# Merge gates through DRAM and a new order of the mixers in a hybrid decoder trunk

## The chip, the cores and the metric

The kernel runs on one core of a Trainium2 chip. The metric is the device time of one execution in microseconds; several runs are taken and the median is compared.

## The reference

Two layers (DEPTH = 2) work on 256 prompt positions and 8 sample sequences of 8 positions, 320 columns in all, of width 1024. Each layer is:

```python
x = x + 0.5 * swiglu_ffn(rmsnorm(x), ...)            # 1024 -> 2 x 2816 -> 1024
h = rmsnorm(x)
q, k, v, g_ret, u, z, xbc, dt, gate_logits = split(h @ w_in)
y_ret = (silu(g_ret) * norm(retention(rotary(q), rotary(k), v, state))) @ ret_w_o   # 4 heads
y_s5  = glu(gelu(grouped complex scan of u) @ s5_w_glu)                              # 64 groups
y_ssd = norm(silu(z) * (ssd(silu(conv(xbc)), softplus(dt), state) + d * xs)) @ ssd_w_o   # 4 groups of 8 heads
gates = sigmoid(gate_logits)                          # 3 x 1024 channels
x = x + (gates[0] * y_ret + gates[1] * y_s5 + gates[2] * y_ssd) @ w_out
x = x + 0.5 * swiglu_ffn(rmsnorm(x), ...)
```

All is float32. The outputs are the activations and the new states of the retention, S5, SSD and convolution branches.

## The kernel before

Activations lie transposed: a tile `t` is 128 channels by 320 positions (53 such buffers). Every large product is made exact enough by splitting both operands into a high and a low part: `stream` (L265) loads weights in pieces of 128x1024 (512 KB) on SP's queue, ScalarE rounds them (`whi`, L278) and VectorE takes the rest (`wlo`, L279), and `proj` (L285) issues three matmuls for each of eight blocks (L292 to L294), so a projection unit is 24 matmuls of 128x320 into one of four PSUM buffers `pp`. The smaller matmuls of the branches go to four PSUM buffers `pb`.

A scheduler sorts the instructions of each engine: it takes the order in which the program emits them as precedence, and issues what is ready by its cost model. `high_priority` moves an instruction forward by a number of places (AHEAD for weight loads and splits, SOON for PSUM evictions). The program emits the mixer with `weave` (L379): a list of main units (projections), and after each unit a share of the steps of the side generators (the branches).

The stages of a mixer, in `layer` (L1278): the opening (time steps `ssd_dt`, S5 inputs `u`, the convolution inputs x of SSD group 0); then, for g = 0 to 3, the SSD group g (`ssd_group`, L588) beside the x of the next group, the z gates (`ssd_gate`, L748) of the group before and that group's part of the SSD output projection (`ssd_part`, L552); retention's q, k and v units stand with the last groups. Then the four retention heads (`ret_head`, L836) run two at a time beside the third merge gate (`g2`), the retention gates (`ret_gate`, L920) and the first merge gates; the S5 blocks (`s5_block`, L1172) run beside all of these from group 2 on. Last come the retention output projection, the second merge gates with `s5_post`, the S5 output projection with its merge, and `w_out`.

A merge gate (`gate`, L1270) is one projection unit and a Tanh; its tile stays in SBUF until the merge. POOL's queue issues, in its order, all loads and stores but the weights': states (L601, L842), row sums that are broadcast (L596), S5 tables (L1183 to L1189), results (L703, L909, L1241, L1256).

Of the kernel before, what the change touches and what calls it, by code (L numbers as in the profile page):

```python
# [40 lines left out]
SOON = 60  # L41
# [3 lines left out]
DTL = 3  # L45
URAW = 6
NPRI = 200
AHEAD = 120
# [105 lines left out]
class Trunk:  # L154
# [270 lines left out]
    DT_STEPS = 5  # L425

    def ssd_dt(self, l, h, r):
        nc, C = self.nc, self.C
        resets = self.tab(7)
        p = self.proj(self.stream("w_dt", l), h)  # L430
# [7 lines left out]
        nc.vector.tensor_scalar(y, y, 0.0, None, op0=ALU.max)  # L438
        z = self.t()
# [9 lines left out]
        dt = self.t()  # L449
        nc.vector.scalar_tensor_tensor(dt, q, 2.0, y, op0=ALU.mult, op1=ALU.add)  # L450
        ea = self.s("ea", [128, 1])
        nc.scalar.activation(ea, self.col(l, "a_log", 0), AF.Exp)
        dta = self.t()
        nc.vector.tensor_scalar(dta, dt, ea, -1.0, op0=ALU.mult, op1=ALU.mult)
        cum = self.t()
        nc.vector.tensor_tensor_scan(cum, resets, dta, initial=0.0, op0=ALU.mult, op1=ALU.add)
        cd = self.dr.tile([128, T], F32, name=self.nm("cd"))
# [6 lines left out]
        nrev = self.t()  # L464
# [6 lines left out]
        w = self.t()  # L471
        nc.scalar.activation(w[:, :128], nrev[:, :128], AF.Exp, scale=-1.0, bias=cum[:, LP - 1:LP])
        nc.scalar.activation(w[:, 128:], nrev[:, 128:], AF.Exp, scale=-1.0)
        nc.vector.tensor_tensor(w, w, dt, op=ALU.mult)
# [10 lines left out]
        yield  # L485
# [4 lines left out]
        yield  # L490
# [95 lines left out]
    SSD_STEPS = 18  # L586

    def ssd_group(self, l, g, xin):  # L588
# [3 lines left out]
        bcs = []  # L592
# [6 lines left out]
        h0 = [self.A(2, 512) for _ in range(4)]  # L599
        for i in range(4):  # L600
            nc.gpsimd.dma_start(out=h0[i], in_=ap["ssm_in"][l][:, g, 2 * i:2 * i + 2])  # L601
# [194 lines left out]
    def ret_v(self, l, h, v, vs):  # L796
# [4 lines left out]
        def unit(nh):  # L801
# [20 lines left out]
            for b in range(2):  # L822
                nc.scalar.activation(vt[:, b], pv[b], AF.Copy)

            nc.scalar.activation(vt[:NS, 2], pv[2][:NS], AF.Copy)
            nc.vector.tensor_tensor(vt[NS:, 2], pv[2][NS:], vt[:NS, 2], op=ALU.add)
            v.append(vt)
            VS = self.A(2, 512, dt=F32R)
            self.spread(self.stack(vt[NS:, 2], "vh"), 0, VS)
            vs.append(VS)  # L830

        return [lambda nh=nh: unit(nh) for nh in range(2)]

    RET_STEPS = 8

    def ret_head(self, l, hd, rot, v, vs, out):  # L836
# [6 lines left out]
        mk, qd = self.tab(2 + hd), self.tab(6)  # L843
        q, k = rot["q", hd], rot["k", hd]
# [66 lines left out]

        pm = self.ps()
# [4 lines left out]
        out[hd] = os, self.rstd(os, 256)  # L917
        yield

    def ret_gate(self, l, h, hd, st, heads):  # L920

        nc = self.nc

        def unit(e):
            pg = self.proj(st, h())
            sg = self.t()
            nc.scalar.activation(sg, pg[:, :T], AF.Silu)
            os, r = heads[hd]
            nc.vector.scalar_tensor_tensor(os[e], sg, self.col(l, "ret_ln_g", 2 * hd + e), os[e], op0=ALU.mult, op1=ALU.mult)
            nc.vector.tensor_tensor(os[e], os[e], r, op=ALU.mult)  # L930

        return [lambda e=e: unit(e) for e in range(2)]
# [237 lines left out]
    S5_STEPS = 8  # L1170

    def s5_block(self, l, Q, ud, yd, blk):  # L1172
# [20 lines left out]
        cs, sn = (rt[:, 512 * i:512 * i + 512].rearrange("p (g k) -> p g k", g=NG) for i in range(2))  # L1193
        yield
# [82 lines left out]

    def layer(self, l):  # L1278
# [28 lines left out]
        rest = xi[NRAW:]
        for m in range(len(ui)):
            rest.insert(2 * m + 1, ui[m])
        self.weave(rest, (dt, self.DT_STEPS - 1 - DTL))  # L1310
# [10 lines left out]
        gu = [[lambda i=i: gs[i].append(self.gate(S[f"t{i}"], h())) for m in range(KD)] for i in range(2)]
        GD = (0, 0, 0, 0, 0, 2, 4, 2)
        GO = [sum(GD[:i]) for i in range(9)]
        G = lambda i: gu[0][GO[i]:GO[i + 1]]
        PL = ((), (), (0,), (1, 2), (3, 4), (5, 6), (7,))
        P = lambda i: [s5(*PL[i])] if PL[i] else []
        self.weave(uu + xu(1) + G(0), [(dt, DTL), ssd(0)], *P(0))
        XK = 2
        mix = lambda a, b: a[:XK] + b + a[XK:]
        self.weave(mix(xu(2), zu(0)) + G(1) + ou(0), ssd(1), *P(1))  # L1330
        self.weave(mix(xu(3), zu(1)) + G(2) + ou(1)[:4] + [self.ret_tabs] + ou(1)[4:], ssd(2), *P(2))
        self.weave(mix(qk, zu(2)) + G(3) + ou(2), ssd(3), *P(3))
        self.weave(vu[:1] + zu(3) + vu[1:] + G(4) + ou(3), *P(4))
        ret = [(self.ret_head(l, hd, rot, v, vs, heads), self.RET_STEPS) for hd in range(RH)]

# [5 lines left out]
        rg = lambda hd: self.ret_gate(l, h, hd, S["g"], heads)  # L1341
        self.weave(g2 + G(5), ret[:2], *P(5))
        self.weave(rg(0) + rg(1) + G(6), ret[2:], *P(6))
        for u in rg(2) + rg(3):
            u()
        yret = [self.split(o) for hd in range(RH) for o in heads[hd][0]]
        for u in G(7):
            u()
# [181 lines left out]
```

## Time and profile before

| | |
|---|---|
| median of 3 runs | 2414.15 us (2404.64 to 2421.31) |
| profiled execution | 2408.9 us |
| its span | 2407.1 us |
| TensorE busy | 2302.3 us (96%) in 15798 matmuls |
| VectorE busy | 1752.1 us (73%) |
| ScalarE busy | 1256.8 us (52%) |
| POOL busy | 392.3 us (16%) |
| mean granted TensorE clock | 0.982 |
| moved by DMA | 439.88 MB, 183 GB/s |

The times of the busy rows are unions: matmuls overlap, so the sum of their single durations (about 0.31 us each) is more than the busy time. A granted clock of 1.00 is 2.4 GHz and 0.50 is 1.2 GHz; means between them are mixtures of the two. Layer 0's mixer lies from 253 to 962 us and layer 1's from 1443 to 2170 us; the rest are the feed-forward parts.

### The profile page before, as it was taken

To read this page: it belongs to the slowest core of one execution; us is meant where nothing else is said; L and a number is where in the kernel's file an instruction comes from. 1 tells how busy PE (TensorE), PEld (TensorE's weight loads), DVE (VectorE), ACT (ScalarE), POOL (GpSimd) and SP (SyncE) were. 2 spreads that over 40 slices of the span, in tenths; PEclk is the share of its full clock that TensorE was granted. 3 is DMA by queue.
4 is the path that set the end of the run, shared out by engine and by line. 5 is a ranking of instruction groups with operands and counts; after the bars stand their busy time and mean duration, and the time that the engine had idled before them with its cause. 6 is when DMAs were issued, how large, how long until landed. Compare 5 with 4: busy or idle time off the path is not lost.

```text
span 2407.1 us, 41311 instructions
## 1 busy us (share of the span) xinstructions
PE 2302.3 (96%) x15798; PEld 2182.7 (91%) x15798; DVE 1752.1 (73%) x3366; ACT 1256.8 (52%) x2281; POOL 392.3 (16%) x762
## 2 busy tenths in 40 slices
PE   7999999989999999999999999899899999999998
PEld 7999887868788999999999999788788889999998
DVE  7989789888765656776877677988786666566564
ACT  4444478767444454444443445788565444544342
POOL 0111233221122100000100113432111321000000
PEclk9999999999999999999999999999999999999999
DMA  5767656664566555555556566665655755555553
GB/s 170 233 211 226 213 173 219 193 226 132 177 221 213 151 161 177 146 165 177 176 177 191 180 210 191 204 208 163 203 160 178 255 191 154 174 151 149 149 149 110
DMA packets 126247, 439.88 MB, mean 183 GB/s; under 512 B 18208, under 2 KB 22016, under 8 KB 126048
## 3 DMA queue, kind: packets, MB, share of 16 engines
q1 hardware_dynamic: 82080, 293.11, 40.4%
q0 software_dynamic: 43968, 144.12, 17.9%
q8 instruction: 124, 2.03, 0.4%
q14 instruction: 75, 0.61, 0.1%
HBM read 373.45 MB, written 65.03 MB: 182 GB/s over the span
## 4 chain that ended last, share of the span: by engine, by line
PE 80%; ACT 6%; DVE 6%; DMA 4%; issue 3%; POOL 1%; SPq 0%; DVEq 0%; ACTq 0%; POOLq 0%
PE pp L292 23%; PE pp L293 23%; PE pp L294 22%; ACT whi L278 2%; DVE wlo L279 1%; DMA t<-in_tabs 1%; ACT B L661 1%; PE pb L1199 1%; PE pb L689 1%; PE pb L348 1%; PE pb L333 1%; PE pb L1247 1%; DMA A<-toep 1%; PE pp L818 1%; PE pb L708 1%
## 5 line engine op out<-in xcount | busy, mean ns | idle before, releaser
L292 PE MATMUL pp<-t,whi 128*128 128x320 f32 x4304 | 1347.5, 314 | 34.0 <-ACT t L363 12.7
L294 PE MATMUL pp<-t,wlo 128*128 128x320 f32 x4304 | 1339.2, 312 | 7.9 <-DVE wlo L279 7.9
L293 PE MATMUL pp<-t,whi 128*128 128x320 f32 x4304 | 1340.6, 312 | 1.1 <-DVE t L303 0.7
L278 ACT ACTIVATE whi<-wraw 128x1024 fp32r<-128x1024 f32 x554 | 585.9, 1058 | 760.5 <-PE pp L293 374.5
L279 DVE TENSOR_TENSOR wlo<-wraw,whi 128x1024 fp32r<-128x1024 f32 x554 | 676.7, 1222 | 260.1 <-ACT whi L278 258.1
L292 PEld LDWEIGHTS pp<-t,whi 128*128 128x128 f32 x4304 | 813.4, 189 | 50.2 <-ACT whi L278 16.2
L294 PEld LDWEIGHTS pp<-t,wlo 128*128 128x128 f32 x4304 | 813.0, 189 | 16.1 <-DVE wlo L279 11.4
L293 PEld LDWEIGHTS pp<-t,whi 128*128 128x128 f32 x4304 | 814.3, 189 | 6.4 <-DVE t L303 1.6
L302 ACT ACTIVATE t<-t 128x320 fp32r<-128x320 f32 x184 | 83.7, 461 | 57.0 <-DVE t L1367 28.9
L303 DVE TENSOR_TENSOR t<-t,t 128x320 fp32r<-128x320 f32 x184 | 88.7, 486 | 22.5 <-ACT t L302 21.7
L526 DVE SCALAR_TENSOR_TENSOR acc<-xpad,cols,acc 128x344 f32<-128x344 f32 x144 | 81.0, 571 | 5.8 <-ACT acc L523 4.5
L403 DVE TENSOR_TENSOR t<-pp,t 128x320 f32<-128x320 f32 x88 | 42.6, 485 | 44.8 <-PE pp L294 39.0
L409 DVE TENSOR_TENSOR t<-t,pp 128x320 f32<-128x320 f32 x88 | 42.6, 484 | 38.6 <-PE pp L294 37.7
L323 ACT ACTIVATE t<-t 128x320 f32<-128x320 f32 x104 | 47.6, 462 | 32.4 <-DVE t L916 16.0
L661 ACT ACTIVATE B<-C,tk 128x128 f32<-128x128 f32 x192 | 63.2, 392 | 0.1
L414 DVE SCALAR_TENSOR_TENSOR t<-pp,t 128x320 f32<-128x320 f32 x64 | 31.2, 488 | 35.2 <-PE pp L294 35.0
L404 ACT ACTIVATE t<-t 128x320 f32<-128x320 f32 x88 | 40.3, 458 | 21.7 <-DVE t L403 21.6
L519 POOL COPY cso<-xpad 128x3 f32<-128x3 f32 x48 | 25.1, 523 | 147.4 <-ACT xpad L514 119.8
L405 DVE TENSOR_TENSOR t<-t,t 128x320 f32<-128x320 f32 x88 | 42.6, 484 | 4.5 <-ACT t L404 4.5
L1111 POOL DMA_DIRECT2D kd<-t x64 | 32.6, 516 | 78.5 <-issue 73.4
L325 DVE TENSOR_TENSOR t<-t,t 128x320 f32<-128x320 f32 x81 | 39.2, 484 | 6.1 <-ACT t L323 6.0
L699 DVE TENSOR_TENSOR A<-A,dec 128x512 f32<-128x512 f32 x64 | 41.9, 683 | 0.3 <-PE pb L689 0.3
(364 smaller groups left out, 2449.0 us busy)
## 6 DMA issues: line engine op xcount, KB each, us to landing
wraw<-in_w_gu SPq DMA_DIRECT2D x176, 512.0 KB, 3.5
wraw<-in_w_down SPq DMA_DIRECT2D x88, 512.0 KB, 3.6
wraw<-in_w_xbc SPq DMA_DIRECT2D x48, 512.0 KB, 3.7
wraw<-in_w_gate SPq DMA_DIRECT2D x48, 512.0 KB, 3.9
A<-in_ssm_in POOLq DMA_DIRECT2D x32, 512.0 KB, 5.4
wraw<-in_w_z SPq DMA_DIRECT2D x32, 512.0 KB, 4.6
out_ssm_s<-A POOLq DMA_DIRECT2D x32, 512.0 KB, 4.0
wraw<-in_ssd_w_o SPq DMA_DIRECT2D x32, 512.0 KB, 3.6
```

The source lines that it names most:

```text
L278: nc.scalar.activation(hi[:, :w], raw[:, :w], AF.Copy)
L279: nc.vector.tensor_tensor(lo[:, :w], raw[:, :w], hi[:, :w].bitcast(F32), op=ALU.subtract)
L292: nc.tensor.matmul(p[:, :T], wh, xh, start=k == 0, stop=False)
L293: nc.tensor.matmul(p[:, :T], wh, xl, start=False, stop=False)
L294: nc.tensor.matmul(p[:, :T], wl, xh, start=False, stop=k == n - 1)
L302: nc.scalar.activation(hi, src, AF.Copy)
L303: nc.vector.tensor_tensor(lo, src, hi.bitcast(F32), op=ALU.subtract)
L323: self.nc.scalar.activation(q, x, AF.Square)
L403: V.tensor_tensor(hid[i], p[:, :T], r, op=ALU.mult)
L405: V.tensor_tensor(hid[i], hid[i], r, op=ALU.mult)
L526: nc.vector.scalar_tensor_tensor(acc[:, :n], xp[:, r:r + n], self.col(l, "conv_w", 4 * i + r), acc[:, :n], op0=ALU.mult, op1=ALU.add)
L661: S.activation(lm[:, e, o:o + 128], bc[:, i0:i0 + 128], AF.Relu, scale=-1.0, bias=tk[:, b, c:c + 1])
```

## The change

- Both sets of eight first and second merge gates are computed where the new order puts them (W0 to W8 of them between the stages of the SSD groups, the rest beside the retention heads), stored to DRAM (`gd`) and loaded again two units before the merge. The eight retention gates go the same way (`sd`) and are loaded by their head, which now also scales and splits its result.
- `ssd_group` loads its row sums two by two and its states in four parts, in a different order of steps; `s5_block` has two empty steps more behind its loads; `ret_head` likewise.
- `ssd_dt` writes into tiles that it already has and has eight steps, three of them in the opening's first units.
- The z gate is 0.5 * (tanh(z/2) + 1) * z instead of Silu.
- `ret_v` is cut into four units for each half. SOON is 600 instead of 60.
- `s5_post` stands beside the retention output projection.

```diff
-SOON = 60
+SOON = 600
-DTL = 3
+DTL = 1
+W0, W1, W2, W3, W4, W5, W6, W7, W8 = 4, 1, 1, 1, 1, 1, 1, 0, 1
+S5P = ((0,), (1, 2), (3, 4), (5, 6), (7,))
...
-        dt = self.t()
+        dt, dta, cum, nrev, w = y, z, q, e, z
...
-        for i in range(4):
+        def sums():
+            i = len(bcs)
             bc = self.pC.tile([128, 2, T], F32, tag="C", name=self.nm("C"))
...
+        def states():
+            i = len(h0)
+            h0.append(self.A(2, 512))
+            nc.gpsimd.dma_start(out=h0[i], in_=ap["ssm_in"][l][:, g, 2 * i:2 * i + 2])
...
         decays(0)
+        sums()
+        sums()
+        yield
+        XW = self.A(2, 512, dt=F32R)
+        self.spread(xh, 0, XW)
         yield
         given(0)
         yield
+        inside(0)
+        states()
+        yield
         update(0)
         yield
-        inside(0)
-        yield
         inside(1)
+        states()
+        yield
...
-                nc.scalar.activation(z, pz[:, :T], AF.Silu)
-            nc.vector.tensor_tensor(ys[i], z, ys[i], op=ALU.mult)
+                nc.scalar.activation(z, pz[:, :T], AF.Tanh, scale=0.5)
+                nc.vector.scalar_tensor_tensor(z, z, 1.0, pz[:, :T], op0=ALU.add, op1=ALU.mult)
+            nc.vector.scalar_tensor_tensor(ys[i], z, 0.5, ys[i], op0=ALU.mult, op1=ALU.mult)
...
+        sgs = [self.fetch(sd[:, 2 * hd + e]) for e in range(2)]
         pm = self.ps()
...
+        r = self.rstd(os, 256)
+        yield
+        for e in range(2):
+            V.scalar_tensor_tensor(os[e], sgs[e], self.col(l, "ret_ln_g", 2 * hd + e), os[e], op0=ALU.mult, op1=ALU.mult)
+            V.tensor_tensor(os[e], os[e], r, op=ALU.mult)
+            out.append(self.split(os[e]))
+        yield
...
+    def fetch(self, src):
+        t = self.t()
+        self.nc.gpsimd.dma_start(out=t, in_=src)
+        return t
+
+    @staticmethod
+    def blend(a, b):
+
+        return [u for _, _, u in sorted([((i + 0.5) / len(x), k, u) for k, x in enumerate((a, b)) for i, u in enumerate(x)],
+                                        key=lambda v: v[:2])]
...
+        def gate(i, m):
+            nc.gpsimd.dma_start(out=gd[i][:, m], in_=self.gate(S[f"t{i}"], h()))
+
+
+        free = [lambda i=i, m=m: gate(i, m) for i in range(2) for m in range(KD)]
+        rg = self.ret_gate(l, h, S["g"], sd)
+        take = lambda n: [free.pop(0) for _ in range(n)]
+        blend = self.blend
+        self.weave(blend(uu + xu(1), take(W0)), [(dt, DTL), ssd(0)])
+        x = xu(2)
+        self.weave(take(W1) + x[:2] + zu(0) + blend(x[2:], take(W2)) + take(W3) + ou(0), ssd(1))
+        x, o = xu(3), ou(1)
+        self.weave(take(W4) + x[:2] + zu(1) + blend(x[2:], take(W5)) + take(W6) + o[:4] + [self.ret_tabs] + o[4:], ssd(2), s5(*S5P[0]))
+        self.weave(take(W7) + qk[:2] + zu(2) + qk[2:5] + take(W8) + blend(qk[5:], ou(2)), ssd(3), s5(*S5P[1]))
+        o = ou(3)
+        self.weave(vu[0] + zu(3) + [vr] + vu[1] + o[:2] + [vr] + o[2:], s5(*S5P[2]))
...
+        self.weave(rg[:4] + g2[:4] + take(n // 2), ret[:2], s5(*S5P[3]))
+        self.weave(rg[4:] + g2[4:] + take(len(free)), ret[2:], s5(*S5P[4]))
         so = self.stream("ret_w_o", l)
+        ys5 = []
+        gs = [self.fetch(gd[0][:, m]) for m in range(2)]
         for m in range(KD):
-            g = gs[0][m]
+            g = gs[m]
+            if m + 2 < KD:
+                gs.append(self.fetch(gd[0][:, m + 2]))
             p = self.proj(so, yret)
             V.scalar_tensor_tensor(g, g, 1.0, p[:, :T], op0=ALU.add, op1=ALU.mult)
             V.tensor_tensor(merged[m], merged[m], g, op=ALU.add)
-        ys5 = []
-        for m in range(KD):
-            gu[1][m]()
             ys5.append(self.s5_post(l, yd, m))
+        gs = [self.fetch(gd[1][:, m]) for m in range(2)]
...
```

## Rows read from the trace of the kernel before

**Rows 1.** Busy time of each engine in stretches; clock, DMA share, GB/s.

```profile
core 0: us, PE busy (x) PEld busy (x) DVE busy (x) ACT busy (x) POOL busy (x), PEclk, DMA share, GB/s
0.00:253.00 253.00, 237.70 (x1702) 233.32 (x1703) 217.28 (x485) 118.32 (x194) 43.76 (x90) 1.00 0.67 211
253.00:322.00 69.00, 63.37 (x394) 59.91 (x393) 50.36 (x94) 36.06 (x69) 19.87 (x47) 0.95 0.62 192
322.00:640.00 318.00, 292.65 (x1932) 257.77 (x1931) 266.10 (x513) 224.07 (x478) 85.47 (x171) 0.95 0.60 192
640.00:822.00 182.00, 173.34 (x1227) 156.05 (x1226) 116.16 (x270) 87.05 (x178) 39.55 (x72) 0.98 0.60 195
...
962.00:1443.00 481.00, 480.82 (x3384) 477.30 (x3383) 358.19 (x689) 212.66 (x324) 39.37 (x73) 1.00 0.59 178
1443.00:1515.00 72.00, 70.05 (x472) 68.55 (x471) 54.69 (x94) 37.32 (x64) 21.75 (x44) 1.00 0.63 188
1515.00:1840.00 325.00, 299.75 (x1979) 263.48 (x1978) 270.19 (x526) 232.18 (x493) 82.74 (x162) 0.95 0.59 188
1840.00:2028.00 188.00, 179.19 (x1295) 163.50 (x1294) 121.88 (x274) 86.87 (x175) 40.57 (x73) 1.00 0.62 199
```

**Rows 2.** The same view in stretches of 2 us at two pauses.

```profile
508.00:510.00 2.00, 0.24 (x1) 0.24 (x2) 2.00 (x8) 2.00 (x3) 0.60 (x2) 0.86 0.57 115
510.00:512.00 2.00, 2.00 (x11) 0.99 (x12) 2.00 (x4) 0.66 (x1) 1.08 (x2) 0.50 0.62 248
...
538.00:540.00 2.00, 0.00 (x0) 0.00 (x0) 1.53 (x3) 0.67 (x2) 0.00 (x0) 1.00 0.91 275
...
542.00:544.00 2.00, 2.00 (x14) 1.86 (x13) 0.17 (x1) 0.94 (x3) 0.00 (x0) 0.50 0.01 4
```

**Rows 3.** TensorE's timeline at the second pause.

```profile
540.83 2.55 PE L1199 MATMUL pb<-t,A 64*128 64x80 f32 x16 [4.46 <-DMA t<-in_s_in]
```

**Rows 4.** Matmuls of projections alone, by stretch: busy time and count.

```profile
962.00:1443.00 481.00, 474.27 (x3200) 1.00 0.59 178
```

**Rows 5.** Groups by line: busy us, mean ns, idle before and its releasers.

```profile
L278 ACT ACTIVATE whi<-wraw 128x1024 fp32r<-128x1024 f32 x554 | 585.9, 1058 | 760.5 <-PE pp L293 374.5 <-issue 349.7 <-PE pp L820 19.7
L1275 ACT ACTIVATE t<-pp 128x320 f32<-128x320 f32 x64 | 27.0, 425 | 1.2 <-PE pp L294 1.2
L757 ACT ACT_TABLE_LOAD x8 | 10.3, 1283 | 0.1
L1199 PE MATMUL pb<-t,A 64*128 64x80 f32 x256 | 26.1, 307 | 12.9 <-issue 5.9 <-DMA t<-in_s_in 4.5 <-DMA t<-ud 2.5
...
L703 POOL DMA_DIRECT2D out_ssm_s<-A x32 | 17.5, 546 | 86.1 <-DVE A L702 86.1
...
L279 DVE TENSOR_TENSOR wlo<-wraw,whi 128x1024 fp32r<-128x1024 f32 x554 | 676.7, 1222 | 260.1 <-ACT whi L278 258.1
L414 DVE SCALAR_TENSOR_TENSOR t<-pp,t 128x320 f32<-128x320 f32 x64 | 31.2, 488 | 35.2 <-PE pp L294 35.0
```

**Rows 6.** ScalarE's timeline at a table load.

```profile
357.89 1.28 ACT L665 ACT_TABLE_LOAD   x1
359.18 0.84 ACT L665 ACTIVATE B<-B 128x768 f32<-128x768 f32 x1
```

**Rows 7.** Timeline of the last head's end in layer 0.

```profile
813.50 0.88 DVE L916 TENSOR_TENSOR t<-t,pb 128x320 f32<-128x320 f32 x2
...
820.53 0.44 ACT L351 ACTIVATE t<-pb 128x320 f32<-128x320 f32 x1 [2.77 <-PE pb L348]
...
821.33 0.55 DVE L929 SCALAR_TENSOR_TENSOR t<-t,cols,t 128x320 f32<-128x320 f32 x1 [1.83 <-ACT t L927]
821.91 0.49 DVE L930 TENSOR_TENSOR t<-t,t 128x320 f32<-128x320 f32 x1
```

**Rows 8.** POOL's waits: us in total, times, longest us.

```profile
POOL out_ssm_s L703 <- DVE A L702: 86.1, 22, 11.7
```

**Rows 9.** DMA issues: KB each, us to landing.

```profile
A<-in_ssm_in POOLq DMA_DIRECT2D x32, 512.0 KB, 5.4
```

More of the change, by code (lines that the diff above doesn't have):

```diff
@@ L422, in ffn @@
         self.weave(main, *sides)
-    DT_STEPS = 5
+    DT_STEPS = 8
     def ssd_dt(self, l, h, r):
@@ L429, in ssd_dt @@
         resets = self.tab(7)
+        ea = self.s("ea", [128, 1])
+        nc.scalar.activation(ea, self.col(l, "a_log", 0), AF.Exp)
         p = self.proj(self.stream("w_dt", l), h)
@@ L448, in ssd_dt @@
         nc.vector.scalar_tensor_tensor(q, q, 1.0, z, op0=ALU.add, op1=ALU.mult)
-        dt = self.t()
+        dt, dta, cum, nrev, w = y, z, q, e, z
         nc.vector.scalar_tensor_tensor(dt, q, 2.0, y, op0=ALU.mult, op1=ALU.add)
-        ea = self.s("ea", [128, 1])
-        nc.scalar.activation(ea, self.col(l, "a_log", 0), AF.Exp)
-        dta = self.t()
         nc.vector.tensor_scalar(dta, dt, ea, -1.0, op0=ALU.mult, op1=ALU.mult)
-        cum = self.t()
         nc.vector.tensor_tensor_scan(cum, resets, dta, initial=0.0, op0=ALU.mult, op1=ALU.add)
+        yield
         cd = self.dr.tile([128, T], F32, name=self.nm("cd"))
@@ L462, in ssd_dt @@
         nc.gpsimd.dma_start(out=ced, in_=ce)
-        nrev = self.t()
         cv = cum[:, :LP].rearrange("p (c t) -> p c t", c=2)
@@ L470, in ssd_dt @@
                                 sv[:, :, LS - 1:LS].to_broadcast([128, NB, LS]), op=ALU.subtract)
-        w = self.t()
+        yield
         nc.scalar.activation(w[:, :128], nrev[:, :128], AF.Exp, scale=-1.0, bias=cum[:, LP - 1:LP])
         nc.scalar.activation(w[:, 128:], nrev[:, 128:], AF.Exp, scale=-1.0)
+        yield
         nc.vector.tensor_tensor(w, w, dt, op=ALU.mult)
@@ L489, in ssd_dt @@
                             in_=ced.rearrange("(g s r) b -> g s (r b)", g=4, s=4)[:, 0].partition_broadcast(128))
-        yield
         cpad = self.pad[1]
@@ L584, in spread @@
             nc.scalar.activation(out[:, hf], p[:, :n], AF.Copy)
-    SSD_STEPS = 18
+    SSD_STEPS = 20
     def ssd_group(self, l, g, xin):
@@ L591, in ssd_group @@
         tk, cd, dec, ec = self.dtq
-        bcs = []
-        for i in range(4):
+        bcs, h0 = [], []
+        def sums():
+            i = len(bcs)
             bc = self.pC.tile([128, 2, T], F32, tag="C", name=self.nm("C"))
@@ L597, in ssd_group @@
             bcs.append(bc)
+        def states():
+            i = len(h0)
+            h0.append(self.A(2, 512))
+            nc.gpsimd.dma_start(out=h0[i], in_=ap["ssm_in"][l][:, g, 2 * i:2 * i + 2])
         B, Cc, *xs = xin
-        h0 = [self.A(2, 512) for _ in range(4)]
-        for i in range(4):
-            nc.gpsimd.dma_start(out=h0[i], in_=ap["ssm_in"][l][:, g, 2 * i:2 * i + 2])
+        sums()
+        sums()
         pc = self.ps()
@@ L620, in ssd_group @@
         hl = self.stack(pt[NS:, 256:384], "bh")
+        cpd = self.pad[g % 2]
+        S.activation(cpd[:, :, :LS], Cc[:, LP:].rearrange("p (b t) -> p b t", b=NB), AF.Copy)
+        yield
+        states()
         BT = []
@@ L628, in ssd_group @@
             BT.append(b4)
-        cpd = self.pad[g % 2]
-        S.activation(cpd[:, :, :LS], Cc[:, LP:].rearrange("p (b t) -> p b t", b=NB), AF.Copy)
-        yield
         xdt = self.B(3, 512)
@@ L645, in ssd_group @@
                     V.tensor_tensor(dst[:, b].rearrange("p (r c) -> p r c", r=8), pv, f, op=ALU.mult)
-            yield
-        XW = self.A(2, 512, dt=F32R)
-        self.spread(self.stack(xws, "xh"), 0, XW)
+            if b < 2:
+                yield
+            if b == 0:
+                states()
+        xh = self.stack(xws, "xh")
         yield
@@ L713, in ssd_group @@
         decays(0)
+        sums()
+        sums()
+        yield
+        XW = self.A(2, 512, dt=F32R)
+        self.spread(xh, 0, XW)
         yield
@@ L716, in ssd_group @@
         yield
+        inside(0)
+        states()
+        yield
         update(0)
         yield
-        inside(0)
+        inside(1)
+        states()
         yield
-        inside(1)
         decays(2)
@@ L799, in ret_v, with unit @@
         sts = []
-        def unit(nh):
+        def unit(nh, part):
             if not sts:
@@ L809, in unit @@
                 sts.append(lh)
-            vt = self.B(3, 512)
-            pv = [self.pps() for _ in range(3)]
-            for k in range(KD):
+            if part == 0:
+                pvs.append([self.pps() for _ in range(3)])
+            pv = pvs[-1]
+            for k in range(2 * part, 2 * part + 2):
                 wh, wl = next(sts[0])
@@ L821, in unit, with rows, ret_head @@
                 nc.tensor.matmul(pv[2], xs, wl, start=False, stop=k == KD - 1)
[L822 to L826, printed above, removed]
+            if 2 * part + 2 < KD:
+                return
+            vt = self.B(3, 512)
+            with self.soon():
+                for b in range(2):
+                    nc.scalar.activation(vt[:, b], pv[b], AF.Copy)
+                nc.scalar.activation(vt[:NS, 2], pv[2][:NS], AF.Copy)
+                nc.vector.tensor_tensor(vt[NS:, 2], pv[2][NS:], vt[:NS, 2], op=ALU.add)
             v.append(vt)
+        def rows():
+            hl = self.stack(v[-1][NS:, 2], "vh")
             VS = self.A(2, 512, dt=F32R)
-            self.spread(self.stack(vt[NS:, 2], "vh"), 0, VS)
+            self.spread(hl, 0, VS)
             vs.append(VS)
-        return [lambda nh=nh: unit(nh) for nh in range(2)]
-    RET_STEPS = 8
-    def ret_head(self, l, hd, rot, v, vs, out):
+        pvs = []
+        return [[lambda nh=nh, i=i: unit(nh, i) for i in range(KD // 2)] for nh in range(2)], rows
+    RET_STEPS = 12
+    def ret_head(self, l, hd, rot, v, vs, sd, out):
         nc, C, ap = self.nc, self.C, self.ap
@@ L843, in ret_head @@
         mk, qd = self.tab(2 + hd), self.tab(6)
+        yield
+        yield
         q, k = rot["q", hd], rot["k", hd]
@@ L864, in ret_head @@
             S.activation(kt[:, b], pt[:, b * 128:(b + 1) * 128], AF.Copy, scale=kd[:, b, hd:hd + 1])
+        kh = self.stack(kt[NS:, 2], "kh")
+        yield
         KT = self.tv(2, 128, dt=F32R)
-        self.spread(self.stack(kt[NS:, 2], "kh"), 1, KT)
-        yield
+        self.spread(kh, 1, KT)
         ys = []
@@ L916, in ret_head, with ret_gate, unit @@
             V.tensor_tensor(os[e], os[e], pm[:, :T], op=ALU.subtract)
-        out[hd] = os, self.rstd(os, 256)
         yield
-    def ret_gate(self, l, h, hd, st, heads):
-        nc = self.nc
[L924 to L932, printed above, removed]
+        r = self.rstd(os, 256)
+        yield
+        for e in range(2):
+            V.scalar_tensor_tensor(os[e], sgs[e], self.col(l, "ret_ln_g", 2 * hd + e), os[e], op0=ALU.mult, op1=ALU.mult)
+            V.tensor_tensor(os[e], os[e], r, op=ALU.mult)
+            out.append(self.split(os[e]))
+        yield
+    def ret_gate(self, l, h, st, sd):
+        nc = self.nc
+        def unit(m):
+            p = self.proj(st, h())
+            g = self.t()
+            with self.soon():
+                nc.scalar.activation(g, p[:, :T], AF.Silu)
+            nc.gpsimd.dma_start(out=sd[:, m], in_=g)
+        return [lambda m=m: unit(m) for m in range(KD)]
     def exp_exact(self, x, n):
@@ L1168, in s5_u @@
         nc.gpsimd.dma_start(out=ud[m].rearrange("t p k -> p t k"), in_=u.rearrange("p (t k) -> p t k", t=CK))
-    S5_STEPS = 8
+    S5_STEPS = 9
     def s5_block(self, l, Q, ud, yd, blk):
@@ L1193, in s5_block @@
         cs, sn = (rt[:, 512 * i:512 * i + 512].rearrange("p (g k) -> p g k", g=NG) for i in range(2))
+        yield
+        yield
         yield
@@ L1305, in layer @@
             xi[m]()
+            if m:
+                next(dt)
         ui = [lambda m=m: self.s5_u(l, S["u"], ud, m, h()) for m in range(NRAW, URAW)]
[L1307 to L1310, printed above, removed]
+        self.weave(self.blend(xi[NRAW:], ui), (dt, self.DT_STEPS - NRAW - DTL))
         ssd = lambda g: (self.ssd_group(l, g, xg[g]), self.SSD_STEPS)
@@ L1317, in layer @@
         rot, v, vs, heads = {}, [], [], {}
-        qk, vu = self.ret_qk(l, h, rot), self.ret_v(l, h, v, vs)
-        gs = [[], []]
+        qk, (vu, vr) = self.ret_qk(l, h, rot), self.ret_v(l, h, v, vs)
         S["t0"], S["t1"] = self.stream("w_gate0", l), self.stream("w_gate1", l)
[L1321 to L1334, printed above, removed]
+        gd = self.dr.tile([2, 128, KD, T], F32, name=self.nm("gd"))
+        sd = self.dr.tile([128, KD, T], F32, name=self.nm("sd"))
+        def gate(i, m):
[12 more added lines that the diff above has]
+        self.weave(vu[0] + zu(3) + [vr] + vu[1] + o[:2] + [vr] + o[2:], s5(*S5P[2]))
+        yret = []
+        ret = [(self.ret_head(l, hd, rot, v, vs, sd, yret), self.RET_STEPS) for hd in range(RH)]
         def gate2(m):
@@ L1340, in layer @@
         g2 = [lambda m=m: gate2(m) for m in range(KD)]
[L1341 to L1348, printed above, removed]
+        n = len(free)
+        self.weave(rg[:4] + g2[:4] + take(n // 2), ret[:2], s5(*S5P[3]))
+        self.weave(rg[4:] + g2[4:] + take(len(free)), ret[2:], s5(*S5P[4]))
         so = self.stream("ret_w_o", l)
+        ys5 = []
+        gs = [self.fetch(gd[0][:, m]) for m in range(2)]
         for m in range(KD):
-            g = gs[0][m]
+            g = gs[m]
+            if m + 2 < KD:
+                gs.append(self.fetch(gd[0][:, m + 2]))
             p = self.proj(so, yret)
@@ L1361, in layer @@
         for m in range(KD):
-            g = gs[1][m]
+            g = gs[m]
+            if m + 2 < KD:
+                gs.append(self.fetch(gd[1][:, m + 2]))
             s = self.gate(so, ys5)
```

## The prediction

> **What bounds the kernel now.** I read the windows by stage first, with borders where the weight loads of a new stage begin. The feed-forward stretch between the two mixers is full: TensorE is busy 480.82 of 481 us at full clock. The stretches that hold the state-space (SSD) groups, 322 to 640 us and 1515 to 1840 us, are not: 292.65 of 318 and 299.75 of 325 us busy, 50.6 us idle together, and the granted clock falls to a mean of 0.95 in both [rows 1]. There VectorE is busy 266.10 and 270.19 us (84% and 83%) and ScalarE about 70%. The retention stretches (640 to 822, 1840 to 2028) idle for 8.7 and 8.8 us, and the openings of the mixers (253 to 322, 1443 to 1515) for 5.6 and 2.0 us [rows 1].
>
> Then the short windows, for what a pause costs. At 508 to 510 us TensorE works 0.24 of 2 us while VectorE and ScalarE are full; the clock is 0.50 in the next 2 us, the lower of the two levels, 1.2 GHz. At 538 to 540 us TensorE stands still, ScalarE nearly, with the DMA engines 91% busy; the clock is 0.50 at 542 to 544 [rows 2]. The second pause, 4.46 us, ends with the load of a block of the S5 scan [rows 3]. [...] The slow clock's share is (1 - 0.95) x (318 + 325) = 32 us in the SSD stretches. What this change can reach in them is 50.6 + 32.2 = 83 us; the openings add 7.6 idle and 3.5 clock (0.05 x 69), the retention stretches 17.5 and 3.6.
>
> **The moved gate units.** A gate unit is 24 matmuls of 128x320. At the feed-forward rate (3200 matmuls in 474.27 us, 0.148 us each [rows 4]) it is 3.56 us of TensorE; it needs one weight split (1.058 us ScalarE, 1.222 us VectorE) and one Tanh (0.425 us) [rows 5]. Before, eight stand in the retention stretches, from the second pair of units on, and eight behind the retention output projection, so none beside an SSD group. After, 4+1+1+1+1+1+1+0+1 = 11 a layer stand between SSD steps, 22 in all: TensorE 78.3 us, VectorE 26.9, ScalarE 32.6.
>
> **The z gate by tanh.** Silu and a product become Tanh and two three-operand operations: 32 more on VectorE at 0.488 us, the row of the like operation that reads PSUM, 15.6 us. The Silu of z had 8 table loads of 1.283 us; Tanh (64 of line 1275) had none, neither near Silu nor elsewhere [rows 5]. So ScalarE loses 10.3 us at most, nothing at least if the next Silu loads in their place. All 32 units lie in the SSD stretches. The Trainium skill (ScalarE: Activation LUTs, "What ACT_TABLE_LOAD costs") puts a switch at 2.66 us with a drain; that would make these eight 21 us, and rival 1 below would end 11 us lower. The trace disagrees on the second half: a load at 357.89 us is followed by the activation at 359.18, 1.29 us later [rows 6].
>
> **Sum for the SSD stretches.** Left in their old places the 22 units cost 78.3 us elsewhere, so old stretch plus units is 643 + 78.3 = 721.3 us. After, TensorE's own work is 592.4 - 32.2 (slow clock) + 78.3 = 638.5 us; VectorE's is 536.3 + 26.9 + 15.6 = 578.8; ScalarE's 456.3 + 32.6 - 10.3 = 478.6. TensorE is the largest. How near it comes is bounded from below by the SSD stretches halved (idle from 8% to 6% and half of the clock kept: (638.5 + 16) / 0.94 = 696, a gain of 25) and from above by the full feed-forward (638.5 / 0.99 = 645, a gain of 76). I take the retention stretches' share, (173.34 + 179.19) / 370 = 0.953, the nearest row as it has the same mix of projections and small matmuls: 670 us, **a gain of 51**. VectorE would be 86% busy, as it is in 0 to 253 us beside a TensorE at 94% [rows 1].
>
> **Loads in parts and empty steps.** Row sums and states come two at a time instead of eight loads at the group's start, and each S5 block waits two empty steps between its loads and its first matmul. S5's first matmuls (line 1199) stand behind late data for 12.9 us in the run [rows 5]. This is part of the 51 where it lies in the SSD stretches; it costs no instruction.
>
> **The retention stretch.** Before, ten and eight units cover the heads, then six units (four gates of retention, two merge gates) stand between the last head and the output projection. After, 21 units cover the heads and none is left behind: the output projection needs the last head's tiles. That head's tail is, from the mean's subtraction at 813.50 to the norm's copy, which ends at 820.97, 7.5 us; two products for each half (0.55 + 0.49) and one split, estimated by a copy and a product (0.44 + 0.49), end it at about 10.5 us [rows 7]. Six of eight input blocks are ready, so 18 matmuls (2.7 us) of the first unit, and as many of a second, can go ahead: 5 us stay open. Bounds: 0 if held-back units fill it, 8 if only the first unit goes ahead. I charge **10 us for two layers**; the idle of 17.5 us stays otherwise.
>
> **The round trip through DRAM.** 48 more transfers of 160 KB a layer: 16 gates and 8 retention gates out, and all back. On POOL's queue 96 issues at 0.546 us, the row of the states' stores [rows 5], are 52 us over 1154 us of these stretches, in which POOL is busy 290 us [rows 1]. A state's load, three times the size, lands in 5.4 us [rows 9]; a gate is fetched two units ahead, 7 us, so I charge nothing. If that cover is gone it is the first fetch of each of two loops, 4 x 5.4 = 22 us; a gain I exclude, as the transfers replace none. [...]
>
> **The time-step chain** reuses its tiles and starts three steps earlier; of the opening's 11 us I take **3** (0 to 11). Giving PSUM evictions more precedence changes no count; it is inside the bounds above.
>
> Sum: -51 + 10 - 3 = -44 on the profiled execution's 2408.9 us (span 2407.1) gives 2365; the median of the runs is 5 us above that execution, so I say **2368 us**.
>
> **Rivals.**
> 1. *The two vector engines are the bound.* For it: at 508 us both are full while TensorE idles [rows 2]. Then the units lengthen what they fill: VectorE's 42.5 us and ScalarE's 22.3 us in a chain make the stretches 643 + 64.8 = 708 us, a gain of 13, less 10 for the tail: 2406 us in the profile's terms, 2411 by the median. The same result comes if the planner, which sorts by readiness, leaves the moved units where they were, so that the change does not do what it says. Against it: VectorE is at 84% over the stretch, and in the pause at 538 us ScalarE is idle for two thirds.
> 2. *POOL's queue turns into the wait (slower).* Every gate store waits in order for its Tanh; behind it stand row sums, states and S5 loads. POOL already waits 3.9 us before a state's store (86.1 us, 22 times) [rows 8]. If TensorE paid 3.9 us for each of 22 stores it would be 86 us against 51 + 3 - 10: 2408.9 + 42 = 2451 us, 2456 by the median. It decides from 2 us per store on. Against it: no instruction is on record as a waiter of the states' loads, which land in 5.4 us [rows 9], and they move by one unit at most.
> 3. *The bursts go as well (larger gain).* If the pause at 538 us and its kind vanish together with the head's uncovered tail, the SSD stretches reach 76, the openings 7 and the retention stretches 6: 2408.9 - 89 = 2320 us, 2325 by the median.
>
> **Chances.** The forecast case 0.55 (2345 to 2395 by the terms), rival 1 0.22, rival 2 0.12, rival 3 0.11. One per cent, 24 us, is about what runs of this kernel tell from no change. The forecast case ends below 2390 nearly always, rival 3 always: faster 0.66; rival 1 and the forecast's upper end: same 0.23; rival 2: slower 0.11. The range reaches to rival 3 and over rival 1: 2318 to 2416.
>
> **What would show it.** Right: the SSD stretches, now with 22 gate units, at about 335 us a layer, TensorE at 95% or more and a clock of 0.98 there; eight fewer table loads; line 1199 without waits; closing projections shorter by 8 units; a pause of some 5 us before the retention output projection. Wrong: VectorE over 90% there with TensorE still at 92%, or SSD matmuls that wait for row sums or states whose issue stands behind a gate store.

## The result and the profile after

The changed kernel takes 2378.76 us (median of 4, 2373.80 to 2385.66) against 2415.28 us beside it: ratio 0.9855, interval 0.9813 to 0.9898. The forecast was 2368; 46 us less was expected and 36.5 came.

The windows by stage of the changed kernel, columns as in [rows 1]; the borders are moved with its weight loads.

```profile
253.00:322.00 69.00, 62.89 (x390) 59.56 (x389) 53.27 (x101) 37.58 (x67) 19.11 (x42) 0.95 0.56 169
322.00:653.00 331.00, 319.76 (x2207) 289.40 (x2206) 277.48 (x528) 223.49 (x490) 91.82 (x192) 0.99 0.67 216
653.00:812.00 159.00, 153.72 (x1052) 138.30 (x1053) 102.84 (x232) 76.78 (x152) 42.89 (x78) 0.98 0.64 213
812.00:862.00 50.00, 44.16 (x302) 40.06 (x301) 31.65 (x73) 24.06 (x46) 15.46 (x26) 0.97 0.53 167
945.00:1425.00 480.00, 479.77 (x3377) 476.30 (x3376) 357.33 (x688) 212.44 (x323) 39.31 (x73) 1.00 0.58 177
1494.00:1823.00 329.00, 317.85 (x2169) 286.28 (x2168) 271.78 (x518) 219.69 (x481) 84.69 (x180) 0.98 0.66 213
1978.00:2029.00 51.00, 45.02 (x298) 40.62 (x298) 31.22 (x72) 24.16 (x46) 15.49 (x26) 0.93 0.50 159
```

The SSD stretches are 331 and 329 us with 11 gate units more each (335 forecast), TensorE at 96.6% (95.3 forecast) and a clock of 0.99 and 0.98. VectorE is at 84% and 83%, as before. The bad places are now the 50 us around the start of the retention output projection: 5.8 and 6.0 us idle.

To compare equal work I cut each mixer at three weight loads on SP's queue: those of the time steps, of the last SSD output part and of the S5 output projection. Layer 0 before, then after (start us, us, queue, line):

```profile
249.49 0.33 SPq L277 DMA_DIRECT2D wraw<-in_w_dt  x1
654.47 13.01 SPq L277 DMA_DIRECT2D wraw<-in_ssd_w_o  x4
879.83 54.85 SPq L277 DMA_DIRECT2D wraw<-in_s_w_glu  x16
```

```profile
249.62 0.33 SPq L279 DMA_DIRECT2D wraw<-in_w_dt  x1
666.54 14.55 SPq L279 DMA_DIRECT2D wraw<-in_ssd_w_o  x4
861.49 55.60 SPq L279 DMA_DIRECT2D wraw<-in_s_w_glu  x16
```

The first part is 405.0 us before and 416.9 after, the second 225.4 and 195.0. With layer 1 (396.0 and 411.3; 222.0 and 192.6) and the 78.3 us of the 22 moved units: **first parts 801.0 + 78.3 - 828.2 = 51.1 us gained; second parts 387.6 - (447.4 - 78.3) = 18.5 us lost.** The rest, the S5 output projections and the feed-forward parts, loses 1.6. That is the span's 31.0 us.

A load stands ahead of its work, and not always by as much. This is ScalarE's split of the piece at the second cut, before and after:

```profile
664.61 1.05 ACT L278 ACTIVATE whi<-wraw 128x1024 fp32r<-128x1024 f32 x1
```

```profile
678.42 1.06 ACT L280 ACTIVATE whi<-wraw 128x1024 fp32r<-128x1024 f32 x1 [1.65 <-issue]
```

It comes 10.1 us behind its load before and 11.9 after. Cut at the splits of the same pieces, the parts are 803.4 and 443.5 us before, 834.4 and 380.2 after: **47.3 gained and 15.0 lost**. So the cut by loads moves some 4 us from one part to the other.

Each part is from one execution. The total of one kernel varies by up to 25 us (before: 2399.55 to 2424.83), but the first parts of kernels that hardly differ there agree better: 828.2 (changed), 828.2 (b1) and 827.3 (c4).

TensorE's group of S5's first matmuls, whose line had 12.9 us of idle in [rows 5]:

```profile
L1238 PE MATMUL pb<-t,A 64*128 64x80 f32 x256 | 24.6, 280 | 0.0
```

ScalarE's two largest groups of table loads, of 34 loads in all (54 before):

```profile
L529 ACT ACT_TABLE_LOAD x12 | 15.4, 1283 | 0.2
L675 ACT ACT_TABLE_LOAD x10 | 12.8, 1283 | 0.2
```

### The profile page after: what moved, and what is told of

It reads as the page before. It is cut to its first block, busy times and chain, and to the rows that moved or that the text cites. A ratio compares the mean times of both kernels' runs of the same rounds, so it can differ in the third digit from the quotient of the medians.

```text
span 2376.1 us, 41534 instructions
## 1 busy us (share of the span) xinstructions
PE 2294.7 (97%) x15798; PEld 2177.9 (92%) x15798; DVE 1754.0 (74%) x3398; ACT 1231.0 (52%) x2261; POOL 439.5 (18%) x858
## 4 chain that ended last, share of the span: by engine, by line
PE 78%; ACT 6%; DVE 6%; issue 5%; DMA 2%; POOL 2%; SPq 0%; DVEq 0%; POOLq 0%; ACTq 0%
PE pp L294 22%; PE pp L296 22%; PE pp L295 22%; DVE wlo L281 2%; ACT whi L280 2%; DMA t<-in_tabs 2%; PE pb L1238 1%; ACT B L671 1%; PE pb L350 1%; PE pb L711 1%; PE pb L718 1%; PE pb L687 1%; PE pp L836 1%; PE pp L837 1%; PE pp L838 0%
## 5 line engine op out<-in xcount | busy, mean ns | idle before, releaser
L280 ACT ACTIVATE whi<-wraw 128x1024 fp32r<-128x1024 f32 x554 | 586.2, 1059 | 779.1 <-issue 388.7
L325 ACT ACTIVATE t<-t 128x320 f32<-128x320 f32 x104 | 47.2, 460 | 25.7 <-DVE t L416 12.2
L407 DVE TENSOR_TENSOR t<-t,t 128x320 f32<-128x320 f32 x88 | 42.7, 485 | 4.5 <-ACT t L406 4.5
L1166 POOL DMA_DIRECT2D pk<-A x16 | 8.8, 552 | 188.4 <-DVE A L1164 188.4
```

The costliest lines, as they stand in the source:

```text
L280: nc.scalar.activation(hi[:, :w], raw[:, :w], AF.Copy)
L325: self.nc.scalar.activation(q, x, AF.Square)
L407: V.tensor_tensor(hid[i], hid[i], r, op=ALU.mult)
```

## The experiments

A is the forecast's account (TensorE work moved to where it waited). "First" and "second" are the two parts above, cut at the loads and summed over both layers, in the profiled execution of each run; moved gates sit in the second part where a kernel has them late. The profiled executions of e1, a2 and c1 are among the slowest of their ten, 14, 6 and 4 us above the median, so their parts are too long by some of that.

| run | median us | ratio to before, interval | span | first | second | table loads |
|---|---|---|---|---|---|---|
| before | 2410 to 2415 | 1 | 2407.1 | 801.0 | 447.4 | 54 |
| changed | 2378.76 | 0.9855 (0.9813 to 0.9898) | 2376.1 | 828.2 | 387.6 | 34 |
| a1 gates late | 2397.12 | 0.9951 (0.9925 to 0.9977) | 2397.7 | 780.8 | 455.9 | 38 |
| a2 z by Silu | 2403.09 | 0.9973 (0.9952 to 0.9995) | 2407.3 | 841.8 | 406.3 | 46 |
| a3 loads at start | 2382.34 | 0.9899 (0.9866 to 0.9932) | 2376.0 | 828.6 | 387.2 | 34 |
| a4 SOON = 60 | 2370.75 | 0.9847 (0.9819 to 0.9875) | 2369.5 | 813.2 | 397.5 | 34 |
| c1 before, tanh | 2407.96 | 0.9999 (0.9978 to 1.0019) | 2410.3 | 786.6 | 463.3 | 42 |
| b1 three units behind | 2355.10 | 0.9773 (0.9748 to 0.9798) | 2356.7 | 828.2 | 369.3 | 34 |
| b2 stores by ScalarE | 2384.05 | 0.9898 (0.9866 to 0.9929) | 2382.1 | 832.1 | 389.7 | 34 |
| b3 stores twice | 2382.03 | 0.9883 (0.9857 to 0.9909) | 2382.7 | 827.0 | 395.7 | 34 |
| c2 SOON = 60, three behind | 2352.84 | 0.9751 (0.9723 to 0.9779) | 2345.2 | 812.8 | 372.4 | 34 |
| c4 five units behind | 2375.07 | 0.9847 (0.9811 to 0.9883) | 2375.4 | 827.3 | 388.2 | 34 |
| e1 extra Silu | 2396.79 | 0.9945 (0.9926 to 0.9963) | 2409.4 | 839.0 | 411.5 | 38 |
| a6 both a3 and a4 | 2372.18 | 0.9834 (0.9809 to 0.9859) | 2365.7 | 811.4 | 396.4 | 34 |

**What moving the gates is worth.** a1:

```diff
-W0, W1, W2, W3, W4, W5, W6, W7, W8 = 4, 1, 1, 1, 1, 1, 1, 0, 1
+W0, W1, W2, W3, W4, W5, W6, W7, W8 = 0, 0, 0, 0, 0, 0, 0, 0, 0
```

> The changed kernel with no gate unit between the SSD groups: all sixteen of a layer stand beside the retention heads, still through DRAM; everything else as changed. Theory A (the gain is TensorE work moved into stretches where it waited): the 51 us that the two layers gain up to the first weight load of the last SSD output part are given back, less some 10 us because the heads are now covered by 32 units instead of 21; 2405 to 2420 us. Rival B (the gain comes from the other edits: loads in parts, eviction precedence, tanh): 2370 to 2385 us, as the same units only stand elsewhere.

The time lies between the two ranges: only two thirds of the gain go (0.9855 to 0.9951). The first parts say why. With no moved unit they are already 20.2 us shorter than before (16.2 cut at the splits); the gates add 780.8 + 78.3 - 828.2 = 30.9 (31.1). So A is right on the larger half, and the other edits have a part of their own that the forecast did not see.

**The tanh.** a2 takes it back, c1 puts it alone into the kernel before:

```diff
-                nc.scalar.activation(z, pz[:, :T], AF.Tanh, scale=0.5)
-                nc.vector.scalar_tensor_tensor(z, z, 1.0, pz[:, :T], op0=ALU.add, op1=ALU.mult)
-            nc.vector.scalar_tensor_tensor(ys[i], z, 0.5, ys[i], op0=ALU.mult, op1=ALU.mult)
+                nc.scalar.activation(z, pz[:, :T], AF.Silu)
+            nc.vector.tensor_tensor(ys[i], z, ys[i], op=ALU.mult)
```

> The changed kernel with the z gate by Silu again (one product instead of two three-operand operations). Theory A: VectorE has 15.6 us less, ScalarE eight or more table loads of 1.28 us again; TensorE is the bound, so within 6 us of the changed kernel, 2373 to 2385 us. Rival B: the table loads between exponentials delayed the weight splits; at 8 loads and what waits behind each, 2388 us or more.

> The kernel before with the z gate by tanh and nothing else. Undoing the tanh in the changed kernel cost 28 us, some 13 of it in the SSD stretches and the rest in the second retention stretch, where the clock stayed at 0.50. Theory A2 (the tanh takes switches of ScalarE's tables out of the SSD stretches, in any order of the mixers): 12 or so table loads fewer than before's 53, the two SSD stretches 10 to 20 us shorter, 2388 to 2400 us. Rival B2 (it only pays beside the moved gates, or the 28 us were the planner's other order): 2403 to 2413 us.

a2 holds rival B: Silu costs 13.6 us in the first parts and 18.7 in the second. How the first comes about, in ScalarE's timeline of a2:

```profile
411.29 1.28 ACT L675 ACT_TABLE_LOAD   x1
412.58 0.85 ACT L675 ACTIVATE B<-B 128x768 f32<-128x768 f32 x1
...
413.81 1.28 ACT L775 ACT_TABLE_LOAD   x1
...
415.80 1.07 ACT L280 ACTIVATE whi<-wraw 128x1024 fp32r<-128x1024 f32 x1
416.89 1.28 ACT L676 ACT_TABLE_LOAD   x1
```

and in its windows of 2 us at the same place:

```profile
414.00:416.00 2.00, 0.79 (x6) 0.53 (x4) 1.25 (x3) 1.99 (x5) 0.12 (x1) 1.00 0.44 149
416.00:418.00 2.00, 0.56 (x2) 0.30 (x2) 1.16 (x2) 1.98 (x2) 0.25 (x2) 1.00 0.00 0
418.00:420.00 2.00, 1.82 (x9) 1.82 (x10) 1.18 (x3) 1.99 (x4) 0.00 (x0) 0.74 0.42 63
420.00:422.00 2.00, 2.00 (x10) 2.00 (x9) 2.00 (x4) 1.50 (x4) 0.00 (x0) 0.50 0.51 199
```

One Silu between the exponentials of one `decays` makes three loads in 6.9 us on a ScalarE that is full; the weight split (L280) stands behind two of them, TensorE idles 2.7 us, and the clock falls to 1.2 GHz. The changed kernel at this place, with one load:

```profile
414.00:416.00 2.00, 2.00 (x15) 2.00 (x15) 1.46 (x4) 2.00 (x6) 1.06 (x2) 1.00 0.82 235
416.00:418.00 2.00, 1.78 (x13) 1.52 (x11) 2.00 (x3) 2.00 (x6) 0.00 (x0) 1.00 0.34 137
```

It is not this one place alone. TensorE's waits for ScalarE's half of the weight split in layer 0's first part (line, releaser, us in total, times, longest), in a2 and then in the changed kernel:

```profile
PE pp L294 <- ACT whi L280: 6.0, 4, 2.1
```

```profile
PE pp L294 <- ACT whi L280: 1.7, 2, 1.3
```

With layer 1 and all lines it is 12.2 us in a2 and 2.4 in the changed kernel; in the old order 9.7 us before and 4.6 in c1. The rest of Silu's price there is mostly slow clock: in layer 0's first part the mean is 0.98 in a2 and 0.99 in the changed kernel, some 4 us of 426.

Of the 18.7 us of the second parts more than half is clock, in one stretch of layer 1 where TensorE is busy for 20 us at half of it:

```profile
1944.00:1964.00 20.00, 20.00 (x72) 16.11 (x72) 8.61 (x21) 6.20 (x15) 2.70 (x5) 0.50 0.27 95
```

c1 finds the same as a2 in the old order, 14.4 us in the first parts (16.7 cut at the splits), and yet no gain, as rival B2 said: its second parts are 15.9 us longer. Layer 1's second part, before and then in c1:

```profile
1838.90:2060.89 221.99, 213.18 (x1523) 197.30 (x1523) 140.69 (x296) 101.86 (x193) 44.32 (x78) 1.00 0.61 194
```

```profile
1832.91:2064.12 231.21, 222.87 (x1525) 205.83 (x1524) 141.51 (x299) 103.29 (x195) 44.15 (x78) 0.96 0.58 186
```

A clock of 0.96 over 231 us is 9.2 us, all that this part is longer. Layer 0 shows how such a stretch begins:

```profile
735.00:743.00 8.00, 3.31 (x26) 2.50 (x28) 3.29 (x10) 1.14 (x5) 0.00 (x0) 0.85 0.33 97
743.00:751.00 8.00, 8.00 (x49) 6.69 (x41) 4.13 (x10) 4.99 (x13) 0.00 (x0) 0.51 0.11 43
```

```profile
738.49 0.42 DVE L853 TENSOR_TENSOR S<-pb,t 128x256 f32<-128x256 f32 x1 [7.93 <-DMA t<-in_tabs]
```

VectorE waits for a table that POOL's queue fetches for a head, TensorE pauses for 4.7 us, then it has half the clock. The planner sorts the whole program, and the second part of c1 has its instructions in another order than before, though the z gates belong to the first. So the total of one run does not price the edit; the part does. e1 did not settle whether the loads alone are the price:

```diff
+                nc.scalar.activation(self.s("dum", [128, 1]), z[:, 0:1], AF.Silu)
```

> The changed kernel with one further Silu on a column of 128x1 behind each Tanh of the z gate, its result not used: 32 tiny activations, and with them the table switches that the Silu form has, while the arithmetic on VectorE stays that of the tanh form. If the switches are what Silu costs beside the moved gates: 10 or more table loads over 33, and 2390 to 2405 us. If it is the order of the plan or VectorE's part: 2374 to 2384 us (32 x 0.2 us on ScalarE, hidden).

The time is in the range that the expectation gives if the loads cost it, but there are 4 loads more, not 10: most extra Silus fell where Silu's set was in place. So this run does not show that ten loads cost the time.

**The loads in parts and the precedence of evictions.** a3 moves all `sums()` and `states()` to the group's start, a4 sets SOON = 60, a6 does both.

> The changed kernel with all four row sums and all four states of a group loaded at the group's start again. Theory A: the loads in parts are worth less than 10 us, 2379 to 2389 us; a pause with the DMA engines full appears near the S5 loads. Rival B: they are the larger part of the gain, 2400 us or more.

> The changed kernel with SOON = 60 again. Theory A: the number of instructions and the bound stay, within 8 us of the changed kernel, 2371 to 2387 us. Rival B: earlier evictions of PSUM are a part of the gain, 2390 us or more, with TensorE waiting for PSUM evictions.

> The changed kernel with both SOON = 60 and the loads at the group's start again: moved gates, tanh, the time-step chain and the empty S5 steps remain. Each of the two alone changed the SSD stretches by less than 5 us. If they are independent: 2370 to 2382 us, the whole gain without them. If each covers for the other: 2388 us or more.

a3 lies in A's range, a6 in that of independence, a4 a quarter of a us below A's: neither edit is part of the gain. For the first parts SOON = 600 is a loss of 15.0 us (a6 and c2 repeat it; the "less than 5 us" for the SSD stretches in a6's expectation was wrong), and 9.9 us of it return in the second; the total does not tell the two values apart. The empty S5 steps and the time-step chain had no run of their own. If SOON's loss is the same beside the gates and without them, something else must make up for it, as the other edits gave 16 to 20 us together and the tanh alone 14 to 17. S5's waits of 12.9 us, which are gone in the changed kernel, a1 and a3, would fit; this is not shown.

**The lost part.** b1 and c4 change what stands behind the heads' weave; b1:

```diff
-        self.weave(rg[4:] + g2[4:] + take(len(free)), ret[2:], s5(*S5P[4]))
+        self.weave(rg[4:] + g2[4:] + take(len(free) - 3), ret[2:], s5(*S5P[4]))
+        for u in take(3):
+            u()
```

> The changed kernel with the last three gate units of a layer behind the retention heads' weave instead of in it, ahead of the retention output projection. Theory C (the last head's uncovered tail is the pause of some 4 us of idle and 2 us of slow clock ahead of that projection in each layer): the pause goes, 6 to 14 us less in all, 2361 to 2369 us on a chip where before takes 2410 us. Rival D (the heads' stretch then is too dense, and loses what the tail gains): 2371 to 2382 us, with the pause gone and others inside the heads' stretch longer.

> The changed kernel with five units (two of the third gate, three merge gates) behind the heads' weave. Theory C says that three units, 10.7 us, already cover the last head's tail of 10.5 us, so two more give nothing: 2353 to 2360 us; rival D says that the weave with six units instead of eight beside two heads is too dense: 2362 us or more, with slow clock inside the heads' stretch.

The pause in windows of 4 us of the changed kernel, layer 0, how its POOL and VectorE come to it, and VectorE's wait at the same place in layer 1:

```profile
840.00:844.00 4.00, 3.15 (x22) 2.65 (x20) 1.64 (x7) 0.00 (x0) 0.00 (x0) 1.00 0.58 204
844.00:848.00 4.00, 1.09 (x7) 0.99 (x8) 2.16 (x10) 1.20 (x3) 0.00 (x0) 1.00 0.00 0
848.00:852.00 4.00, 3.85 (x14) 3.15 (x13) 1.58 (x3) 2.42 (x4) 3.21 (x6) 0.57 0.38 97
```

```profile
837.60 0.55 POOL L1373 DMA_DIRECT2D gd<-t  x1 [1.64 <-ACT t L1314]
838.14 0.54 POOL L1319 DMA_DIRECT2D t<-sd  x1
```

```profile
842.79 0.55 DVE L953 SCALAR_TENSOR_TENSOR t<-t,cols,t 128x320 f32<-128x320 f32 x1 [2.25 <-DMA t<-sd]
...
847.74 0.95 DVE L305 TENSOR_TENSOR t<-t,t 128x320 fp32r<-128x320 f32 x2
...
2010.51 0.55 DVE L953 SCALAR_TENSOR_TENSOR t<-t,cols,t 128x320 f32<-128x320 f32 x1 [2.65 <-DMA t<-sd]
```

The tail runs from 838.16 (the subtraction) to 848.69 with the last split: 10.5 us, the figure of [rows 7]. But that estimate had no fetch in it, and here VectorE stands 2.25 us for the retention gate's tile (`t<-sd`), whose fetch was issued at 838.14, right behind a gate store that waited for its Tanh; in layer 1 it is 2.65 us. TensorE loses 3.9 us idle and (1 - 0.57) x 4 = 1.7 of clock, 5.6 us; in layer 1 it is 6.1:

```profile
2008.00:2020.00 12.00, 7.64 (x41) 6.76 (x40) 5.13 (x17) 3.87 (x7) 3.50 (x7) 0.86 0.30 97
```

With three units behind, b1's windows:

```profile
840.00:844.00 4.00, 4.00 (x30) 4.00 (x29) 1.89 (x4) 1.06 (x1) 4.00 (x7) 1.00 0.87 253
844.00:848.00 4.00, 4.00 (x29) 4.00 (x29) 1.73 (x3) 1.57 (x2) 3.47 (x7) 1.00 1.04 341
848.00:852.00 4.00, 2.72 (x17) 2.20 (x16) 2.59 (x5) 3.80 (x6) 1.84 (x3) 1.00 0.95 299
```

The pause shrinks to 1.3 us at full clock, and the second parts are 369.3 us, what equal work took before (447.4 - 78.3 = 369.1): the whole loss is gone. The two pauses were 11.7 us of these 18.3. The heads too stand in another order in b1; that the rest came from the missing cover is not shown. C's sign holds, with more gain than its range (2355 against 2361 to 2369). With five behind, D holds: the pause stands inside the heads' stretch, in c4's windows:

```profile
810.00:820.00 10.00, 5.27 (x36) 3.75 (x35) 8.70 (x21) 6.26 (x16) 0.55 (x1) 0.82 0.37 105
820.00:830.00 10.00, 9.97 (x55) 8.53 (x55) 4.52 (x9) 2.46 (x6) 2.71 (x5) 0.84 0.34 116
```

**The round trip.** b2 has `nc.scalar.dma_start` for the stores; b3 adds a second store behind each `gd` store.

> The changed kernel with the stores of the merge and retention gates issued from ScalarE's queue, where the Tanh runs, instead of POOL's. POOL then no longer waits for a Tanh (102 us in 19 waits now, one of 27 us that holds the last head's gate and the first merge gates). If that wait is on the path in the retention stretches: 6 to 15 us less, 2360 to 2369 us on a chip where before takes 2410 us. If it is hidden: 2370 to 2380 us; ScalarE pays 48 issues.

> The changed kernel with each merge gate stored twice, to a second place in DRAM too: 32 more issues on POOL's queue, each right behind the other store, 5 MB more. If the round trip is hidden, within 4 us of the changed kernel (2371 to 2379 us on a chip where before takes 2410 us). If POOL's queue or the traffic is a price on the path (rival 2 of the prediction), 32 issues of 0.55 us are 17 us and more: 2388 us or more.

b3 lies between its two ranges, and its interval overlaps that of the changed kernel. 22 of 32 extra stores stand in the first parts and cost nothing there (827.0 against 828.2); the second parts of the profiled execution are 8.1 us longer. So the round trip is hidden in the SSD stretches; that the 8.1 us are its price around the heads is not shown by one execution.

b2 is 4 us above the upper one of its ranges, and its interval overlaps that of the changed kernel too. It takes the late fetch away: VectorE does not wait for `t<-sd` at the last head of either layer, the tail is 8.3 us (841.58 to 849.92 in layer 0), and the pause in layer 0 is 2.5 us at full clock. But in layer 1's retention stretch 3.7 us of pauses are followed by half the clock for 20 us, so the total gains nothing:

```profile
846.00:854.00 8.00, 5.51 (x33) 4.38 (x32) 4.53 (x10) 4.93 (x7) 3.99 (x7) 1.00 0.28 68
...
1954.00:1962.00 8.00, 4.33 (x36) 3.15 (x35) 4.08 (x10) 3.02 (x9) 2.57 (x5) 0.94 0.60 188
1962.00:1982.00 20.00, 20.00 (x73) 16.71 (x74) 3.77 (x7) 2.17 (x6) 3.25 (x6) 0.51 0.39 131
```

What POOL waits for (line, releaser, us in total, times, longest), in the changed kernel and then in b2:

```profile
POOL gd L1373 <- ACT t L1314: 102.4, 19, 26.6
```

```profile
POOL out_ret_p L931 <- ACT t L930: 81.3, 8, 19.4
```

Rid of the wait for the Tanh, the queue waits for the heads' results instead.

**The best version.** c2:

> The changed kernel with SOON = 60 and with the last three gate units behind the heads' weave. If the two gains add (3 us in the median and 6.6 us of span for SOON, 20 us for the tail): 2346 to 2354 us where before takes 2410. If SOON's few us were only another order of the heads that the tail now sets anyway: 2352 to 2358 us.

At 0.9751 it has the lowest ratio of both kernels and all runs; its time is in both ranges and its interval overlaps b1's, so SOON's share is not shown.

## Why the prediction was right, and where not

- *Gain in the SSD stretches, 51 us, and 3 in the openings:* 47 to 51 measured in the first parts, openings included, and the signs hold (TensorE 96.6%, clock 0.98 to 0.99). But it is made of 31 us of gates and 16 to 20 of other edits. Of these the forecast had booked the tanh (14 to 17 us) and SOON (15 us lost) at nothing, and the loads in parts gave nothing. So it is in part luck that the figure is so close.
- *The z gate by tanh:* the step that failed in kind. It was booked as 15.6 us more of VectorE, hidden, and at most 10.3 less of ScalarE, hidden too. It is worth 14 to 17 us in the first parts, in both orders, since weight splits came late behind table loads and TensorE waited for them. 12 loads fewer (46 to 34), not 8: the exponentials' own loads go too. VectorE's added work did not undo the gain; its own price was not measured.
- *The retention stretch, 10 us charged:* mis-sized, 15 to 18.5. The two pauses ahead of the output projection are as charged (5.6 and 6.1 us), though with a fetch in the tail that the estimate did not have, which is luck. The rest lies elsewhere in the second parts, pauses between the heads among it, for which "the idle of 17.5 us stays otherwise" was wrong; in b1 all of the loss is gone.
- *The round trip, nothing charged:* right in the SSD stretches (b3). At the last head of both layers the fetch came late, by 2.25 and 2.65 us, behind a gate store that waited for its Tanh: rival 2's mechanism, in two places. Without it (b2) the tail is 2.2 us shorter.
- *The opening, 3 us:* idle 6.1 us in layer 0, 5.6 before; no gain to see. *S5's empty steps:* the sign holds, line 1199's 12.9 us went to 0.0; no run tested the steps alone.
- *Rival 1* is ruled out as a bound of the whole stretch: VectorE stays at 84% and the units fit. At single places ScalarE did hold TensorE up, as the tanh shows.

## What to carry to other kernels

Move matmul work from full stretches into those where TensorE waits, and count what it leaves uncovered: here three units behind a tail of 10.5 us were right, not none and not five. Price an activation that switches tables by what stands behind it in ScalarE's order, not by its 1.28 us. Where a planner sorts the whole program, compare stages of equal work, since one stage's gain can be lost in the next by another order.

## What the runs showed of the hardware

What a pause costs in clock had no fixed price. In c1, 4.7 us idle at 735 to 743 us were followed by 8 us at 0.51, which is 3.9 us of full clock lost. In b2, 3.7 us idle at 1954 to 1962 us were followed by 20 us at 0.51, 9.8 us lost, with TensorE busy throughout. In the kernel before, 2.5 us idle in layer 1's retention stretch cost no clock:

```profile
1887.00:1891.00 4.00, 1.51 (x21) 0.82 (x21) 3.10 (x10) 1.84 (x4) 0.00 (x0) 1.00 0.70 256
1891.00:1895.00 4.00, 4.00 (x38) 3.87 (x39) 2.55 (x8) 3.00 (x9) 0.00 (x0) 1.00 0.45 131
```

A table load took 1.283 us, and the next activation stands right behind it (411.29 and 412.58 in a2); before the 12 loads of line 529 ScalarE was idle for 0.2 us in all.
